# Where buffers lie in SBUF: weights on multiples of 256 bytes, activations 192 bytes past one

## The chip, the core and the metric

The kernel runs on one core of one Trainium2 chip. The metric is device time in microseconds of one execution, lower is better. Before the change it is 1898.5 us, the median of three runs (1892.57 to 1910.38).

## What is computed

Two transformer blocks over 256 tokens of width 1024, all in fp32. The first has two layers, each a token mixer and a convolutional FFN; the second is one layer with three kinds of attention over latent and context tokens, followed by a mixture of 32 experts. Cut to what matters:

```python
def first_block(x, ...):
    h = x
    for layer in range(DEPTH):                     # 2
        h = h + _token_mixer(_rmsnorm(h, norm1[layer]), w_in[layer], ...)   # xn @ w_in, attention, pooling, w_a, w_b, w_o
        h = h + _conv_ffn(_rmsnorm(h, norm2[layer]), w_up[layer], ..., w_down[layer])
    return _rmsnorm(h, norm_f)

def second_block(x, c, ctx, ...):
    mod_l = silu(c) @ w_ada + b_ada                # modulation, also for the context
    pl, pc = hl @ w_in, hc @ w_in                  # latent and context tokens
    ...                                            # hgrn2, rwkv7, neighbourhood attention
    xl = xl + g1l * (concat(a_lat, b_lat, c_lat) @ w_out)
    return xl + g2l * hierarchical_moe(h2l, ...)   # 32 experts, gate, up and down
```

## The kernel before

A linear layer keeps fp32 accuracy by splitting both factors into a high part in the format fp32r and the remainder. Activations are split once and kept as two tiles: xg (the normed input, two tiles), po, at and mgt in the mixer, hid in the FFN, hc for the context tokens, hl for the latent tokens, mx for the last projection. Weights are split as they arrive: `load` (line 338) brings a tile of 128 x 1024 through SP's queue into pool wr (three buffers), ACT writes its high part wh (line 348), DVE the remainder wl (line 349), and `mm3` issues three matmuls for each of eight slices of 128 rows: wh with the high activation (line 355), wh with the low one (356), wl with the high one (357). Weights are the stationary operand and activations move, 256 columns a matmul, 24 matmuls a weight tile. In `lin_tm` (w_v, w_i, w_nv) it is the other way about: activations are stationary and the weight moves, 512 or 256 columns.

The order of work is that of the program. Stages by time: mixer of layer 0 to 295 us, FFN-up to 492, FFN-down to 553; layer 1: mixer to 846, FFN-up to 1009, FFN-down to 1096; the second block's latent work to 1416; the experts from there. A generator of background work (`pump`) puts pieces of the second block's context work between them: `ada` (w_ada), `context_h` and `context1` in layer 0, `na_table` in FFN-down of layer 0 (a loop over eight heads of a load, two GpSimd operations and a store with two buffers), `ada` and `context2` in layer 1. Expert weights come in 96 tiles of 2 MB through SP's queue (line 1755), as the pools of the second block give their space back.

SBUF is given out by pools: those on the left are stacked upwards from the bottom, those with `side="right"` downwards from the top, tiles in a pool in the order of their first use, everything rounded up to 32 bytes. wh is two pairs of buffers (hi, lo); from the first FFN to the last a third pair, pool wh1 on the right side, takes every third weight tile (`s.whs = s.whs * 2 + [...]`). The addresses that follow from the sizes, with their place modulo 256 bytes (the slices of a tile are a multiple of 256 bytes apart, so that all slices share it):

```
tile(s)                      first byte(s) before               mod 256     after, by the diff
wr (w), wh, wl               34368, 46656, 54848 ...            64          0
wh1 (third pair)             142816, 146912                     224         0
xg, po / qk, mgt, hid / at   167904, 176096 / 184288 / 221152   224         192
hc (context)                 63040, 71232                       64          192
hl (latent)                  146176, 154368                     0           192
mx (high, low)               30144, 32256                       192, 0      128, 192
activation less weight:      xg, po, mgt, hid, at with wh 160, with wh1 0;
                             hc with wh 0, with wh1 96; hl with wh 192; mx with wh 128 and 192
```

## Time and profile before

| | |
|---|---|
| median of three runs | 1898.5 us (1892.57 to 1910.38) |
| the profiled execution | 1901.4 us |
| its span, first to last instruction | 1899.6 us |
| TensorE busy | 1746.7 us of the span |
| VectorE busy | 1097.6 us |
| ScalarE busy | 691.1 us |
| bytes read from HBM | 429.40 MB |
| mean granted TensorE clock | 0.960 |

PE is TensorE's matmuls, PEld its weight loads (they overlap the matmuls), DVE is VectorE, ACT ScalarE, POOL GpSimd, SP SyncE. A line number L355 is one of the kernel's. Matmuls are pipelined and their ends are modelled, so the length of one (0.28 us) is longer than the interval from its start to the next one's start; rates are read from starts.

### The profile page before, as it was taken

What the parts mean: (1) busy time and instruction counts of PE and PEld (TensorE: products, weight loads), DVE (VectorE), ACT (ScalarE), POOL (GpSimd) and SP (SyncE); (2) the same over time, 40 slices, a digit from 0 to 9 for tenths busy, and PEclk for the clock granted to TensorE, in tenths of its full rate; (3) what the DMA queues carried; (4) which work ended last, traced back from release to release, by engine and by line L of the source; (5) the groups of instructions that cost most, each with busy time, mean ns of one, the idle gap of its engine ahead of it and who ended that gap; (6) DMA issues with size and microseconds to landing.
All of it is one profiled execution on the core that took longest, in us unless ns stands there. A gap on an engine that the chain in (4) does not pass through costs nothing.

```text
span 1899.6 us, 37672 instructions
## 1 busy us (share of the span) xinstructions
PE 1746.7 (92%) x15846; PEld 1494.9 (79%) x15846; DVE 1097.6 (58%) x2087; ACT 691.1 (36%) x1078; POOL 148.3 (8%) x295
## 2 busy tenths in 40 slices
PE   7999999999989999999999979989998889878776
PEld 6879999999988889999999978976776555534443
DVE  5558568998545456588997579883544211211111
ACT  3346445654443355454553335421532000000000
POOL 2600000000230000000000001120001000000000
PEclk9999999999999999999999989975998999999999
DMA  9855455556667867454443443320339999999997
GB/s 306 262 186 165 162 190 183 180 176 212 213 223 264 284 215 230 149 165 136 155 158 128 138 156 127 111 68 11 111 148 380 426 427 425 426 427 425 426 425 290
DMA packets 94705, 441.14 MB, mean 232 GB/s; under 512 B 23796, under 2 KB 26388, under 8 KB 81728
## 3 DMA queue, kind: packets, MB, share of 16 engines
q1 hardware_dynamic: 90496, 432.17, 61.9%
q0 software_dynamic: 2224, 5.19, 1.1%
q8 instruction: 126, 2.06, 0.5%
q10 hardware_dynamic: 1808, 1.30, 0.2%
q14 instruction: 51, 0.42, 0.1%
HBM read 429.40 MB, written 9.20 MB: 231 GB/s over the span
## 4 chain that ended last, share of the span: by engine, by line
PE 57%; DMA 18%; DVE 6%; issue 2%; ACT 1%; POOL 1%; ACTq 0%; SPq 0%; POOLq 0%; DVEq 0%
PE g L355 8%; PE g L357 8%; PE g L356 8%; DMA we<-in_w_exp_up 6%; DMA we<-in_w_exp_gate 4%; DMA we<-in_w_exp_down 4%; PE g L1929 3%; PE acc L1953 2%; PE acc L357 2%; PE acc L355 2%; PE acc L356 2%; DVE wl L349 1%; PE g L1946 1%; PE sj L355 1%; PE sj L356 1%
## 5 line engine op out<-in xcount | busy, mean ns | idle before, releaser
L349 DVE TENSOR_TENSOR wl<-w,wh 128x1024 fp32r<-128x1024 f32 x347 | 428.1, 1235 | 244.0 <-ACT wh L348 238.9
L348 ACT ACTIVATE wh<-w 128x1024 fp32r<-128x1024 f32 x347 | 366.6, 1059 | 508.8 <-PE g L356 229.0
L355 PE MATMUL g<-xg,wh 128*128 128x256 f32 x1472 | 420.0, 285 | 13.1 <-ACT wh L348 13.0
L357 PE MATMUL g<-xg,wl 128*128 128x256 f32 x1472 | 419.2, 285 | 2.9 <-DVE wl L349 2.7
L356 PE MATMUL g<-xg,wh 128*128 128x256 f32 x1472 | 416.7, 283 | 0.5 <-DVE xg L504 0.4
L355 PEld LDWEIGHTS g<-xg,wh 128*128 128x128 f32 x1472 | 279.9, 190 | 20.0 <-ACT wh L348 13.9
L357 PEld LDWEIGHTS g<-xg,wl 128*128 128x128 f32 x1472 | 279.7, 190 | 12.6 <-DVE wl L349 5.5
L356 PEld LDWEIGHTS g<-xg,wh 128*128 128x128 f32 x1472 | 279.8, 190 | 4.7 <-issue 2.7
L1929 PEld LDWEIGHTS g<-we,xt 128*32 128x32 f32 x4096 | 109.7, 110 | 47.2 <-issue 27.1
L1929 PE MATMUL g<-we,xt 128*32 128x128 f32 x4096 | 126.4, 274 | 16.1 <-DMA we<-in_w_exp_up 15.3
L1935 DVE SCALAR_TENSOR_TENSOR hd<-hd,g 128x128 f32<-128x128 f32 x32 | 9.2, 288 | 216.0 <-ACT hd L1934 216.0
L1953 PE MATMUL acc<-dn,S 128*128 128x512 f32 (+1 forms) x264 | 120.6, 590 | 0.0
L1950 DVE TENSOR_TENSOR dn<-g,g2r 128x512 f32<-128x512 f32 (+1 forms) x66 | 44.6, 675 | 92.2 <-PE g L1946 90.0
L1946 PE MATMUL g<-we,ht 128*32 128x512 f32 (+1 forms) x528 | 69.7, 650 | 26.8 <-DMA we<-in_w_exp_down 17.7
L1934 ACT ACTIVATE hd<-g 128x128 f32<-128x128 f32 x32 | 8.9, 277 | 212.5 <-PE g L1929 212.5
L1953 PEld LDWEIGHTS acc<-dn,S 128*128 128x128 f32 x264 | 46.7, 192 | 41.8 <-issue 40.7
L1918 POOL TENSOR_SCALAR gr<-G,comb 128x128 f32<-128x128 f32 x64 | 38.0, 606 | 502.1 <-PE g L1922 354.3
L1924 ACT ACTIVATE S<-g 128x256 f32<-128x256 f32 x32 | 12.3, 384 | 155.9 <-PE g L1922 155.9
L355 PE MATMUL sj<-hl,wh 128*128 128x256 f32 x200 | 58.8, 294 | 6.7 <-ACT wh L348 5.5
L357 PE MATMUL sj<-hl,wl 128*128 128x256 f32 x200 | 58.0, 291 | 1.0 <-DVE wl L349 0.9
L356 PE MATMUL sj<-hl,wh 128*128 128x256 f32 x200 | 58.7, 293 | 0.1
L1946 PEld LDWEIGHTS g<-we,ht 128*32 128x32 f32 x528 | 15.5, 114 | 54.0 <-issue 40.5
(801 smaller groups left out, 3614.1 us busy)
## 6 DMA issues: line engine op xcount, KB each, us to landing
w<-in_w_in SPq DMA_DIRECT2D x135, 512.0 KB, 4.0
we<-in_w_exp_gate SPq DMA_DIRECT2D x32, 2048.0 KB, 38.5
we<-in_w_exp_up SPq DMA_DIRECT2D x32, 2048.0 KB, 39.1
we<-in_w_exp_down SPq DMA_DIRECT2D x31, 2048.0 KB, 35.4
w<-in_w_up SPq DMA_DIRECT2D x88, 512.0 KB, 3.3
wa<-in_w_ada SPq DMA_DIRECT2D x48, 512.0 KB, 5.4
w<-in_w_down SPq DMA_DIRECT2D x44, 512.0 KB, 3.4
w<-in_w_v SPq DMA_DIRECT2D x24, 512.0 KB, 3.4
```

The costliest lines, as they stand in the source:

```text
L348: s.nc.scalar.activation(hi, t, AF.Copy)
L349: s.nc.vector.tensor_tensor(lo, t, hi, op=OP.subtract)
L355: mm(out, w[0], x[0], start=first, stop=False, skip_group_check=sk)
L356: mm(out, w[0], x[1], start=False, stop=False, skip_group_check=sk)
L357: mm(out, w[1], x[0], start=False, stop=last, skip_group_check=sk)
L1918: nc.gpsimd.tensor_scalar(gr[:, i], G[:, i, e % 4, None, :].to_broadcast([128, 4, 32]), s.comb[:, i, e:e + 1], None, op0=OP.mult)
L1924: nc.scalar.activation(S, p[:, :T], AF.Copy)
L1929: nc.tensor.matmul(p[32 * j:32 * j + 32, q * 128:(q + 1) * 128], xt[:, k, (e % 4) * 32:(e % 4) * 32 + 32], w[:, k, j * 128:(j + 1) * 128], ...
L1935: nc.vector.scalar_tensor_tensor(hd[:, 0], hd[:, 0], 1.0, p[:, 0:128], op0=OP.add, op1=OP.mult)
L1946: nc.tensor.matmul(p[32 * c:32 * c + 32, :w], ht[:, c * 32:(c + 1) * 32], wd[:, c, q * w:(q + 1) * w], start=True, stop=True, tile_positio ...
L1950: nc.vector.tensor_tensor(dn, p[:, :w], s.g2r[:, q * w:(q + 1) * w], op=OP.mult)
L1953: nc.tensor.matmul(y[i][q * w // 512][:, o:o + w], S[:, i * 128:(i + 1) * 128], dn, start=(more and e == 0), stop=(e == 31), skip_group_ch ...
```

## The change

It alters where tiles lie, and no operation. `pad0` (128 bytes) is put at the bottom of the left side and `pad1` (224 bytes) at the top of the right side. vecs, the first constants, mean, zero, one1, mod, g1m and g2m become slices of one tile `small` whose size is a multiple of 256 bytes; lbt, hw0, ha0, wrt and brt become slices of a longer consts1. Pool sq gets a small tile `pads`, pool s1 one of 192 bytes at its beginning (`shift`) and one of 64 at its end (`unshift`), pool hcp one of 192 at its beginning. With that wr, wh and wh1 begin at a multiple of 256, and xg, po, qk, mgt, hid, at, hc and hl 192 bytes past one (the right column of the table above).

```diff
@@ -121,6 +121,7 @@
     _VOFF[(_n, _l)] = _o
     _o += _k
 NVEC = _o
+NSMALL = -(-(NVEC + _NC[0] + 123) // 64) * 64
 
 
 def _cols(w, tiles=None):
@@ -301,34 +302,44 @@
 
     def setup(s):
         nc = s.nc
+
+        s.pool("pad0").tile([128, 32], F32, name="pad0")
+        s.pool("pad1", side="right").tile([128, 56], F32, name="pad1")
         s.cp = s.pool("const")
         s.left, s.lw = ExitStack(), ExitStack()
         s.b2 = s.pool("b2", ctx=s.left)
         s.open_ps("1")
         s.dr = s.pool("dr", space=DRAM)
         s.hT = s.cp.tile([128, 8, T], F32, name="hT")
-        s.vecs = s.cp.tile([128, NVEC], F32, name="vecs")
+        small = s.cp.tile([128, NSMALL], F32, name="small")
+        cut = [0]
+
+        def take(n):
+            cut[0] += n
+            return small[:, cut[0] - n:cut[0]]
+        s.vecs = take(NVEC)
+        s.consts = [take(_NC[0]), s.b2.tile([128, -(-(_NC[1] + 344) // 64) * 64], F32, name="consts1")]
         nc.scalar.dma_start(s.vecs, s.a["vecs"])
         nc.sync.dma_start(s.hT[:, :4], s.a["xT"][:, :4])
         s.sq = s.pool("sq", bufs=2, ctx=s.left)
+        s.sq.tile([128, 16], F32, name="pads")
         s.wr = s.pool("wr", bufs=3, ctx=s.lw)
         s.whs = [s.pool("wh", bufs=2, ctx=s.lw)]
         s.first = s.wsplit(s.a["w_in0"][8], 8)
         nc.sync.dma_start(s.hT[:, 4:], s.a["xT"][:, 4:])
-        s.consts = [(s.b2 if i else s.cp).tile([128, _NC[i]], F32, name=f"consts{i}") for i in range(2)]
         nc.scalar.dma_start(s.consts[0], s.a["consts0"])
         s.ones = s.cp.tile([128, 128], F32, name="ones")
         nc.vector.memset(s.ones, 1.0)
-        s.mean = s.cp.tile([128, 1], F32, name="mean")
+        s.mean = take(1)
         nc.vector.memset(s.mean, 1.0 / D)
-        s.zero = s.cp.tile([128, 1], F32, name="zero")
+        s.zero = take(1)
         nc.vector.memset(s.zero, 0.0)
-        s.one1 = s.cp.tile([128, 1], F32, name="one1")
+        s.one1 = take(1)
         nc.vector.memset(s.one1, 1.0)
         s.ident = s.c("ident")
-        s.mod = s.cp.tile([128, 48, 2], F32, name="mod")
-        s.g1m = s.cp.tile([128, 2, 8], F32, name="g1m")
-        s.g2m = s.cp.tile([128, 8], F32, name="g2m")
+        s.mod = take(96).rearrange("p (k i) -> p k i", i=2)
+        s.g1m = take(16).rearrange("p (i k) -> p i k", i=2)
+        s.g2m = take(8)
 
 
 
@@ -492,6 +503,10 @@
                     t2[:, None, ::-1].to_broadcast([128, 8, 16]),
                     m2[:, :, None].to_broadcast([128, 8, 16]), op=OP.add)
 
+    def shift(s, pool, k):
+
+        pool.tile([128, k // 4], F32, name="shift")
+
     def norm_begin(s, gn, gl):
 
         s.nx = ([s.s1.tile([128, 8, T], F32R, name=f"xg{q}", tag=f"xg{q}") for q in range(2)], gn, gl)
@@ -513,6 +528,8 @@
         v = s.s1.tile([128, 2, 1536], F32, name="v", tag="v")
         att = s.s1.tile([128, 2, 4, T], F32R, name="at", tag="at")
         at = [att[:, q_] for q_ in range(2)]
+        if l == 0:
+            s.s1.tile([128, 16], F32, name="unshift")
         ps = [s.pair([w_in[8 + m] if l or m else s.first, w_in[9 + m]], x) for m in (0, 2)]
         rc, rows = s.token_r()
         rb = s.bc2(rows)
@@ -713,6 +730,7 @@
         nc = s.nc
         with ExitStack() as ctx:
             s.s1 = s.pool("s1", ctx=ctx, side="right")
+            s.shift(s.s1, 192)
             s.fp = s.pool("fp", bufs=2, ctx=ctx, side="right")
             bd = s.bd = s.dr.tile([128, 4096], F32, name="biasd")
             c1 = [ExitStack(), ExitStack()]
@@ -728,7 +746,7 @@
             for k in range(8):
                 s.norm_tile(k)
             s.bias_tables()
-            nc.sync.dma_start(s.consts[1], s.a["consts1"])
+            nc.sync.dma_start(s.consts[1][:, :_NC[1]], s.a["consts1"])
             nc.gpsimd.dma_start(bd, s.bias.rearrange("p h i c -> p (h i c)"))
             for l in range(2):
                 s.mixer(l)
@@ -779,7 +797,7 @@
         nc.vector.tensor_copy(s.identr, s.ident)
 
         l = s.col("hgrn_lb_logits_2", None, 4)
-        e = b2.tile([128, 3, 4], F32, name="lbt")
+        e = s.consts[1][:, _NC[1]:_NC[1] + 12].rearrange("p (a b) -> p a b", a=3)
         nc.vector.tensor_tensor(e[:, 0], l, l, op=OP.subtract)
         nc.scalar.activation(e[:, 0], e[:, 0], AF.Exp)
         nc.vector.reciprocal(e[:, 1], e[:, 0])
@@ -787,17 +805,17 @@
         nc.vector.tensor_tensor(e[:, 0], e[:, 1], e[:, 1], op=OP.subtract)
         nc.vector.tensor_scalar(e[:, 1], e[:, 0], -1.0, 1.0, op0=OP.mult, op1=OP.add)
         s.lb, s.lb1 = e[:, 0], e[:, 1]
-        s.hw0 = b2.tile([128, 4], F32, name="hw0")
+        s.hw0 = s.consts[1][:, _NC[1] + 12:_NC[1] + 16]
         nc.vector.tensor_scalar(s.hw0, s.col("rwkv_w0_2", 0, 4), 0.5, None, op0=OP.mult)
-        s.ha0 = b2.tile([128, 4], F32, name="ha0")
+        s.ha0 = s.consts[1][:, _NC[1] + 16:_NC[1] + 20]
         nc.vector.tensor_scalar(s.ha0, s.col("rwkv_a0_2", 0, 4), 0.5, None, op0=OP.mult)
         s.hS = [b2.tile([128, 2, 128], F32, name=f"hS{d}") for d in range(2)]
         s.rH = [[b2.tile([128, 128], F32, name=f"rH{d}{j}") for j in range(2)] for d in range(2)]
         for t in s.hS + s.rH[0] + s.rH[1]:
             nc.gpsimd.memset(t, 0.0)
         s.scp = b2.tile([128, 8, 32], F32, name="scp")
-        s.wrt = b2.tile([128, 8, 36], F32, name="wrt")
-        s.brt = b2.tile([128, 36], F32, name="brt")
+        s.wrt = s.consts[1][:, _NC[1] + 20:_NC[1] + 308].rearrange("p (k c) -> p k c", k=8)
+        s.brt = s.consts[1][:, _NC[1] + 308:_NC[1] + 344]
         s.nkv, s.rxd = s.dram("nkv", 2048), s.dram("rxd", 4096)
 
     def dram(s, n, k):
@@ -1511,6 +1529,7 @@
 
         nc = s.nc
         s.hcp = s.pool("hcp", ctx=s.chc)
+        s.shift(s.hcp, 192)
         hi, lo = s.hc = [s.hcp.tile([128, 8, T], F32R, name=f"hc{q}", tag=f"hc{q}") for q in range(2)]
         for q in range(2):
             xc = s.load(s.a["ctxT"][:, 4 * q:4 * q + 4].rearrange("p k t -> p (k t)"))
```

## Rows read from the trace of the kernel before

**Rows 1.** The page: span, and busy time (share) and instructions by engine.
```profile
span 1899.6 us, 37672 instructions
PE 1746.7 (92%) x15846; PEld 1494.9 (79%) x15846; DVE 1097.6 (58%) x2087; ACT 691.1 (36%) x1078; POOL 148.3 (8%) x295
```
**Rows 2.** Busy time by stage: stretch, its length, engines, granted clock, DMA share, GB/s.
```profile
0.00:100.00 100.00, 86.52 (x724) 75.74 (x724) 53.94 (x98) 35.58 (x52) 40.90 (x76) 1.00 0.89 287
100.00:295.00 195.00, 188.85 (x1363) 177.46 (x1364) 129.73 (x208) 102.51 (x149) 0.72 (x10) 0.98 0.52 171
295.00:492.00 197.00, 193.07 (x1562) 189.98 (x1561) 174.90 (x315) 110.72 (x148) 1.75 (x26) 0.99 0.56 188
492.00:553.00 61.00, 57.57 (x467) 56.00 (x466) 26.25 (x21) 22.02 (x22) 27.45 (x24) 1.00 0.70 213
553.00:846.00 293.00, 288.20 (x2284) 260.34 (x2283) 180.29 (x280) 136.87 (x194) 3.13 (x20) 1.00 0.67 223
846.00:1009.00 163.00, 159.90 (x1355) 158.38 (x1353) 152.48 (x282) 88.03 (x129) 3.60 (x24) 0.99 0.46 151
1009.00:1096.00 87.00, 86.80 (x742) 86.49 (x742) 50.22 (x90) 26.98 (x34) 1.49 (x3) 1.00 0.40 132
1096.00:1416.00 320.00, 298.82 (x1932) 251.09 (x1932) 227.72 (x538) 125.70 (x230) 31.20 (x48) 0.85 0.29 98
1416.00:1885.00 469.00, 381.04 (x5384) 235.68 (x5383) 99.11 (x255) 41.16 (x121) 38.02 (x64) 0.96 0.99 416
```
**Rows 3.** The page: the chain that ended last, by engine and by line.
```profile
PE 57%; DMA 18%; DVE 6%; issue 2%; ACT 1%; POOL 1%; ACTq 0%; SPq 0%; POOLq 0%; DVEq 0%
PE g L355 8%; PE g L357 8%; PE g L356 8%; DMA we<-in_w_exp_up 6%; DMA we<-in_w_exp_gate 4%; DMA we<-in_w_exp_down 4%; PE g L1929 3%; PE acc L1953 2%; PE acc L357 2%; PE acc L355 2%; PE acc L356 2%; DVE wl L349 1%; PE g L1946 1%; PE sj L355 1%; PE sj L356 1%
```
**Rows 4.** Timeline of SP from 1415 us: start, length, queue, line, operation.
```profile
1416.29 0.33 SPq L1755 DMA_DIRECT2D we<-in_w_exp_down  x1
```
**Rows 5.** The page: costliest groups, busy time and mean ns, then idle time before.
```profile
L355 PE MATMUL g<-xg,wh 128*128 128x256 f32 x1472 | 420.0, 285 | 13.1 <-ACT wh L348 13.0
```
**Rows 6.** Timeline of PE in the FFN-up stage of layer 0: four matmuls' starts.
```profile
399.77 0.28 PE L356 MATMUL g<-xg,wh 128*128 128x256 f32 x1
...
401.33 0.28 PE L357 MATMUL g<-xg,wl 128*128 128x256 f32 x1
401.45 0.28 PE L355 MATMUL g<-xg,wh 128*128 128x256 f32 x1
...
406.97 0.28 PE L357 MATMUL g<-xg,wl 128*128 128x256 f32 x1
```
**Rows 7.** Timeline of PE, latent stage: first and last of 68 matmuls.
```profile
1120.15 0.28 PE L356 MATMUL sj<-hl,wh 128*128 128x256 f32 x1
...
1128.04 0.28 PE L357 MATMUL sj<-hl,wl 128*128 128x256 f32 x1
```
**Rows 8.** Timeline of PE, latent stage: first and last of 114 matmuls.
```profile
1135.86 0.28 PE L355 MATMUL sj<-hl,wh 128*128 128x256 f32 x1
...
1148.67 0.28 PE L357 MATMUL sj<-hl,wl 128*128 128x256 f32 x1
```
**Rows 9.** Line 355 alone by stage: stretch, length, PE and PEld, clock, DMA.
```profile
0.00:100.00 100.00, 55.27 (x192) 36.93 (x192) 1.00 0.89 287
```
**Rows 10.** Busy time in the middle of FFN-up of layer 1, as rows 2.
```profile
900.00:950.00 50.00, 50.00 (x430) 50.00 (x429) 49.03 (x84) 26.61 (x36) 0.39 (x6) 1.00 0.47 157
```
**Rows 11.** The chain in order of time from 495 us: start, length, what.
```profile
500.32 4.18 DMA z<-in_na_rpb
...
541.46 5.82 DMA z<-in_na_rpb
...
554.58 5.92 DMA w<-in_w_in
```
**Rows 12.** Timeline from 294 us: a reader and a later writer of xg.
```profile
294.69 0.28 PE L355 MATMUL g<-xg,wh 128*128 128x256 f32 x1
...
296.81 0.49 ACT L503 ACTIVATE xg<-hT,vecs 128x256 fp32r<-128x256 f32 x1
```

## The prediction

> **What bounds the kernel now.** I read the page's busy row first: TensorE is busy nine tenths of the span [rows 1], but a busy PE is not yet a bound. The table by stage says where it is one [rows 2]. It has three kinds of stretch. Up to 1096 us (the two layers of the first block) PE works without a break and DVE trails it, closely in the two stages at 295 and 846 us. From 1096 to 1416 us small matmuls of the second block follow one another at a clock of 0.85 on average. From 1416 to 1885 us the DMA share is 0.99: the expert weights stream in, and nothing but their bytes sets the pace. The chain of waits agrees [rows 3]: 57% PE, 18% DMA, and the largest PE groups are the three lines of `mm3`. The expert stream is let go at 1416 us by an issue that stands in SP's queue behind the second block [rows 4]; so what is saved before 1416 us moves the whole stream forward, and what is saved after it is worth nothing.
>
> The change issues no operation more or less, so the question is how fast the matmuls of lines 355 to 357 follow one another. Each has 256 columns; the groups give its modelled length, 285 ns [rows 5], which overlaps the next. What counts is the interval from start to start, and the reader gets it from two rows and the number between them.
>
> **The interval depends on two addresses.** Write "distance" for the position of the moving tile (activation) less that of the stationary tile (weight), modulo 256 bytes; the table of addresses above gives both. In one FFN-up stage, with the same xg throughout, a weight buffer of pool wh1 (distance 0) gives 13 intervals in 1.56 us, exactly 120.0 ns each; from 401.45 us the next buffers belong to wh (distance 160), and 47 intervals take 5.52 us, 117.4 ns [rows 6]. Only the weight buffer changed; engine, stage and neighbours did not. The latent stage of the second block already has distance 192, the one the change makes everywhere. There I find two steady beats: 67 intervals in 7.89 us, 117.8 ns [rows 7], and 113 intervals in 12.81 us, 113.4 ns [rows 8]. A run keeps its beat until PE next has to wait. Of the 180 intervals of these two runs, the longest of the stage, 113 are fast; I take two thirds, so 2/3 x 113.4 + 1/3 x 117.8 = 114.9 ns is the mean I expect at distance 192.
>
> **The change, part by part.** *Weights to 0, activations to 192.* By the loops, the first mixer has 68 weight tiles of 24 such matmuls (the 12 tiles of w_v are 512 wide and have the weight as moving operand), all at distance 160: 1632 matmuls, each 117.4 - 114.9 = 2.5 ns shorter. From the first FFN on the three pairs of buffers take turns, one at distance 0 and two at 160: (5.1 + 2 x 2.5)/3 = 3.4 ns. The context projections (14 tiles, mostly distance 0) gain about 5 ns. The sum on PE alone:
> mixer 0: 1632 x 2.5 = 4.1 us (576 of them before 100 us, from 192 of line 355 [rows 9]: 1.4 us; the rest 2.7);
> FFN-up 0 with the context: 1056 x 3.4 + 336 x 5 = 5.3;
> FFN-down 0: 528 x 3.4 = 1.8;
> mixer 1: 1632 x 3.4 = 5.5;
> FFN-up 1: 1056 x 3.4 = 3.6;
> FFN-down 1: 1.8. Together 22.1 us.
> The hl and mx matmuls keep their distances (192; 128 and 192) and are worth nothing.
>
> How much of it reaches the end is read stage by stage [rows 2]. Before 100 us the DMA share is 0.89 and weights set part of the pace: half, 0.7. Mixer 0 after that has DVE idle for a third: all, 2.7. FFN-up 0 has DVE at 174.9 of 197 us: half, 2.7. FFN-up 1 has 152.5 of 163, and 49.0 of 50 us in its middle [rows 10]: a PE that is 3% faster wants more than DVE has there, so wl, which PE needs, comes late next: half, 1.8. FFN-down 0 ends with the chain of `na_table` from 500 to 554 us (DMA, POOL, DMA, eight heads), behind which the w_in loads of the next layer wait on SP [rows 11]: nothing. Mixer 1 and FFN-down 1 in full: 5.5 and 1.8. Sum 15.2 us of 22.1.
>
> *Bounds.* If every run took the slow beat (117.8), distance 160 loses 0.4 ns and distance 0 gains 2.2: -0.7 + 4800 x 0.47 ns + 336 x 2.2 ns = 2.3 us, of which the same share is 1.6. If every run took the fast beat (113.4): 1632 x 4.0 + 4800 x 4.9 + 336 x 6.6 = 32.3 us, of which 22. I choose the mixture, since rows 7 and 8 are the very distance.
>
> *The w_v and w_nv matmuls* (512 columns, weight moving) go from distance 96 or 0 to 64; there are some 340, and with 7 ns, the largest spread of rows 6 to 8, either way they are worth at most 2.4 us; I take 0. *fp32 matmuls*: about 1,350 records remain before 1096 us (the rows of the seven stages less three times line 355's share); at 7 ns they would be worth 9 us up or down; I take 0, since in most of them both operands lie in pools that move together. *Pads, `small`, the tail of consts1*: no instruction, no DMA and no queue position is added; 56 to 192 bytes each, so no pool is pushed out. If `small` brought a wait, the DVE instruction that writes mod would hold everything behind it (see the rivals). *DMA into shifted tiles*: the expert stream has 0.99 of its engines and cannot get faster; bound 0 to 1% of 469 us, 5 us, taken as 0.
>
> The profiled execution took 1901.4 us (span 1899.6 and 1.8 around it), 2.9 us above the median of the runs shown. 1901.4 - 15.2 = 1886; against the median, 1898.5 - 15.2 = 1883. I forecast 1883.
>
> **A rule against the change.** The row shows two intervals, 120.0 and 117.4, that differ by the weight buffer's place alone [rows 6]. The Trainium skill, page "SBUF — State Buffer", section "Who interferes with whom", says that TensorE reads the moving operand and the next weights through two independent ports and that it never waits on anyone. By that rule no placement matters and the sum is 0; by the rows it is 15 us. The rows speak against it, within one stage. The page "TensorE: Matmul & The Clock Gate", section "Back-to-back issue gap", puts an isolated matmul of 256 columns at 256/2.4 + 2.5 = 109 ns; as an estimate from it, 6,768 matmuls at 109 would give some 60 us on PE, but no run of rows 6 to 8 gets there.
>
> **Rivals.**
> *A. The fast beat everywhere.* In the layers the runs are longer than in the latent stage, and once all buffers share one distance a run crosses from tile to tile without a jolt. If the fast beat is the one that lasts, 22 us: 1876. For it: the longest run of the latent stage is the fast one [rows 8]. Against: the slow one is just as steady for 67 intervals [rows 7].
> *B. Little or nothing arrives.* Either placement is not what sets the interval (the skill's rule above as a mechanism: ports independent, latent stage faster for another reason), then 1898; or the slow beat wins or DVE, nearly full in two stages [rows 2, 10], takes back what PE gains: 2 to 8 us, 1890 to 1897. Against the first stands the switch within one stage [rows 6].
> *C. Slower: waits through `small`.* mod, vecs, ident and the constants now lie in one tile. If order were kept for the tile as a whole, each of the six writes of mod (line 842) and the two of g1m would wait for all reads of ident and vecs before it, on PE behind up to a pair of weight tiles: 48 x 0.12 = 5.8 us a time, 8 times 46 us, less 15: 1929. It turns into a loss from three such waits on. Against: order goes by slices: PE reads the first slices of xg at 294.69 while ACT writes later slices of the same tile at 296.81 [rows 12].
>
> **Chances.** Forecast (both beats, 10 to 20 us) 0.50; A (20 to 30 us) 0.24; B 0.20; C and anything else that is slower 0.06. A measurement of this kernel tells about 1%, 19 us, from no change (its runs lie 18 us apart). Faster by over 1% means more than 19 us: A and a small part of the forecast, 0.30. Slower by over 1% is C, 0.05. Within 1%: 0.65. The range reaches from 1868 (A, with the fp32 bound partly in its favour) to 1899 (nothing arrives); it leaves out the rest of the fp32 bound and C. The likeliest case alone: 1878 to 1889.
>
> **What would show it.** Right: the mean of lines 355 to 357 falls from 285 ns towards 276 to 281; in FFN-up intervals of 113.4 or 117.8 and no 120.0 any more; the expert stream starts 12 to 18 us before 1416; DVE's busy share in FFN-up 1 nears all of it, with idle time of PE before line 357; `na_table` still takes 55 us. Wrong: intervals as before (rule of independent ports); PE waiting on DVE by more than 8 us in the layers (B); waits before line 842 and before readers of ident (C); a longer stretch at half clock between 1096 and 1416 us, which would hide any of it.

## The result and the profile after

The changed kernel takes 1878.1 us (median of six runs, 1872.9 to 1882.6) beside 1895.5 us for the kernel before (six runs too; the 1898.5 ahead of the prediction is the median of three of them): a ratio of 0.9885, 95% interval 0.9839 to 0.9930. Run twice more, unaltered, on other occasions, it gave 0.9892 (0.9845 to 0.9939) and 0.9902 (0.9868 to 0.9935). The medians differ by 17.4, 22.9 and 20.0 us. The forecast was 15.2 us (1883), with 1868 to 1899 as the range. Single executions can fall into a slower state with a lower granted clock, as two of e10's twelve did; e10's time below is the median of the other ten.

The page of the changed kernel: span, busy time by engine, and the groups that answer to [rows 1, 5]. Its lines 366, 367, 368 are the 355, 356, 357 of before, 359 and 360 the two halves of the split.

```profile
span 1876.3 us, 37673 instructions
PE 1726.2 (92%) x15846; PEld 1476.6 (79%) x15846; DVE 1096.1 (58%) x2087; ACT 691.3 (37%) x1078; POOL 149.5 (8%) x295
...
L366 PE MATMUL g<-xg,wh 128*128 128x256 f32 x1472 | 417.6, 284 | 13.2 <-ACT wh L359 13.2
L368 PE MATMUL g<-xg,wl 128*128 128x256 f32 x1472 | 416.8, 283 | 4.1 <-DVE wl L360 3.8
L367 PE MATMUL g<-xg,wh 128*128 128x256 f32 x1472 | 414.1, 281 | 0.0
```

Same operations, 20.5 us less busy PE. The mean lengths of the three groups hardly move (285, 283 and 285 ns before for lines 355, 356 and 357; 284, 281 and 283 now); a length includes a modelled end. The intervals from start to start, which carry the argument, can't be seen here.

They can in the timeline of PE, FFN-up stage of layer 0 (start, length, line, operation): first and last of two unbroken runs of the changed kernel.

```profile
337.08 0.28 PE L367 MATMUL acc<-hc,wh 128*128 128x256 f32 x1
...
352.83 0.28 PE L368 MATMUL g<-xg,wl 128*128 128x256 f32 x1
...
366.06 0.28 PE L367 MATMUL acc<-hc,wh 128*128 128x256 f32 x1
...
384.68 0.28 PE L366 MATMUL acc<-hc,wh 128*128 128x256 f32 x1
```

The first holds 139 intervals in 15.75 us, 113.3 ns each; the second 158 in 18.6 us, 117.8 each. They are the two beats of [rows 7, 8], and both runs cross from hc to xg and from weight tile to weight tile without a change. The 120.0 of [rows 6] is gone. Over all of the about 6,900 unbroken intervals at distance 192 and full clock the mean is 115.1 ns, and the same for the layers and the context alone. In the profile before it was 117.8 at distance 160 (about 4,550) and 119.6 at distance 0 (about 1,760), together 118.3.

Busy time by stage of the changed kernel, columns as in [rows 2], with stretches cut at the new boundaries; the last row is the middle of FFN-up 1, as [rows 10].

```profile
0.00:100.00 100.00, 86.67 (x732) 75.62 (x733) 56.95 (x102) 36.87 (x54) 42.08 (x76) 1.00 0.90 288
...
292.00:488.00 196.00, 190.82 (x1573) 187.63 (x1572) 173.83 (x314) 108.84 (x145) 1.75 (x26) 0.99 0.57 192
...
840.00:1001.00 161.00, 157.80 (x1347) 156.35 (x1347) 149.51 (x278) 85.70 (x124) 3.58 (x24) 0.98 0.45 148
...
886.00:936.00 50.00, 50.00 (x443) 50.00 (x442) 49.93 (x87) 27.50 (x38) 0.52 (x8) 1.00 0.49 161
```

In the middle of FFN-up 1 PE does 443 matmuls in 50 us where it did 430; DVE goes with it, 87 operations for 84, and now has 49.93 us of the 50.

SP's timeline at the release of the expert stream (answers to [rows 4]), and the chain of `na_table` in order of time (answers to [rows 11]; start, length, what).

```profile
1394.95 0.33 SPq L1774 DMA_DIRECT2D we<-in_w_exp_down  x1
```
```profile
492.71 6.70 DMA z<-in_na_rpb
...
532.62 6.20 DMA z<-in_na_rpb
...
546.19 6.12 DMA w<-in_w_in
```

The stream starts 21.3 us earlier. The chain from the first table load to the next layer's w_in takes 53.5 us (54.3 before): it began 7.6 us earlier, and the w_in load behind it came 8.4 us earlier.

**Where the time came from.** To mark the stages I take the start of the last or first matmul that reads a certain tile, in two profiles of the kernel before (the second is the run e8) and three of the kernel after (e7 and e12). Lengths in us, one value for each profile:

| stage | before | after | gain of the means | forecast |
|---|---|---|---|---|
| mixer 0 | 284.7, 283.4 | 278.8, 279.9, 279.3 | 4.7 | 3.4 |
| FFN-up 0 | 197.4, 197.7 | 195.2, 194.7, 196.2 | 2.2 | 2.7 |
| FFN-down 0 and wait for w_in | 72.6, 77.0 | 72.6, 73.5, 73.4 | 1.6 | 0 |
| mixer 1 | 284.4, 285.3 | 279.2, 279.3, 279.7 | 5.5 | 5.5 |
| FFN-up 1 | 160.5, 164.1 | 157.4, 161.1, 161.0 | 2.5 | 1.8 |
| FFN-down 1 | 84.9, 87.4 | 85.3, 86.0, 85.9 | 0.4 | 1.8 |
| latent, first to last hl | 158.0, 160.1 | 157.5, 157.7, 157.9 | 1.3 | 0 |
| latent, last hl to first mx | 125.2, 109.5 | 120.5, 109.5, 106.5 | (clock) | 0 |

Up to the latent stage that is 16.9 us. The two mixers are steady from profile to profile, within 1.3 us; the FFN stages vary by up to 4.4 us for the same kernel. The last row is no effect of the change, as e7 and e8 show.

Much of the spread of the FFN stages is the clock. FFN-up 1 in the first profile before and in e8, the same kernel, then in the first profile after and in e7 (columns as in [rows 2]; the clock is the third number from the end):

```profile
849.00:1009.60 160.60, 157.50 (x1333) 155.86 (x1331) 150.08 (x278) 87.25 (x127) 3.60 (x24) 0.99 0.46 151
```
```profile
853.30:1017.40 164.10, 161.00 (x1332) 159.27 (x1330) 150.66 (x278) 87.19 (x127) 3.59 (x24) 0.97 0.45 149
```
```profile
835.60:993.00 157.40, 154.20 (x1332) 152.54 (x1330) 149.83 (x278) 87.25 (x127) 3.58 (x24) 0.99 0.47 156
```
```profile
837.30:998.40 161.10, 158.12 (x1333) 156.26 (x1331) 150.38 (x279) 87.31 (x127) 3.59 (x24) 0.96 0.45 153
```

PE ran at 1.2 GHz for 3.4, 11.4, 3.4 and 12.0 us of these, and there an interval takes 213 ns, so about half of that time is lost. An estimate with half of it taken off: FFN-up 1 is 158.8 and 158.4 us before, 155.7, 155.1 and 154.8 after, a gain of 3.4; FFN-down 1 is 84.9 and 84.6 before, 83.6, 83.5 and 83.5 after, a gain of 1.2; FFN-up 0 gains 2.7. The first part of the latent stage gains nothing (146.3 and 145.7 before; 146.3, 146.3 and 146.6 after), so its 1.3 us go with the clock.

### The profile page after: what moved, and what is told of

Its sections match the earlier page's. It is cut to its first block, busy times and chain, and to the rows that moved or that the text cites. A ratio compares the mean times of both kernels' runs of the same rounds, so it can differ in the third digit from the quotient of the medians.

```text
span 1876.3 us, 37673 instructions
## 1 busy us (share of the span) xinstructions
PE 1726.2 (92%) x15846; PEld 1476.6 (79%) x15846; DVE 1096.1 (58%) x2087; ACT 691.3 (37%) x1078; POOL 149.5 (8%) x295
## 4 chain that ended last, share of the span: by engine, by line
PE 55%; DMA 19%; DVE 7%; issue 2%; ACT 1%; POOL 1%; SPq 0%; ACTq 0%; POOLq 0%; DVEq 0%
PE g L366 8%; PE g L368 8%; PE g L367 8%; DMA we<-in_w_exp_up 6%; DMA we<-in_w_exp_gate 4%; DMA we<-in_w_exp_down 4%; PE g L1948 3%; PE acc L1972 2%; PE acc L368 2%; PE acc L366 2%; PE acc L367 2%; DVE wl L360 2%; DMA w<-in_w_in 1%; PE g L1965 1%; DMA z<-in_na_rpb 1%
## 5 line engine op out<-in xcount | busy, mean ns | idle before, releaser
L366 PEld LDWEIGHTS g<-xg,wh 128*128 128x128 f32 x1472 | 279.7, 190 | 19.8 <-ACT wh L359 13.8
L367 PEld LDWEIGHTS g<-xg,wh 128*128 128x128 f32 x1472 | 279.9, 190 | 4.2 <-issue 2.7
```

The lines of the kernel that those rows point to most:

```text
L366: mm(out, w[0], x[0], start=first, stop=False, skip_group_check=sk)
L367: mm(out, w[0], x[1], start=False, stop=False, skip_group_check=sk)
```

## The experiments

All ratios are to runs of the kernel before on the same chip. Mean intervals are worked out from the starts in each run's trace: three-product matmuls of 256 columns in the layers and the context, unbroken, at full clock.

**e1: matmuls alone.** A stream with nothing beside it, at 14 pairs of places.

```python
for rep in range(5):
    for wo, xo in PAIRS:          # offsets of weights and activations
        p = ps.tile([128, 512], F32, name="p", tag="p")   # one buffer
        ... 16 x mm3 on hi/lo[wo + ...], x0/x1[xo + ...]
        nc.vector.tensor_scalar(z[...], p[...], 0.0, None, op0=OP.mult)
```

> This kernel leaves out the whole computation and writes zeros: it holds only runs of 48 fp32r matmuls in the pattern of mm3, with nothing beside them, at 14 pairs of places (weight, activation, in bytes past a multiple of 256), each five times, with a short wait before every run. Theory D (the distance activation minus weight, modulo 256, sets the interval): start-to-start 120.0 ns at distance 0, about 117.4 at 160, two beats of 113.4 and 117.8 at 192, and the pairs (64,0), (128,64), (32,224), which are also at 192, as (0,192). Rival P (two independent ports, placement is nothing, the intervals of the kernel come from other engines beside PE): one interval for all 14 pairs, under 113 ns. Rival Q (the absolute place of the weight counts): (64,0) and (128,64) differ from (0,192).

Timeline of PE, e1: first and last matmul of 39 intervals at distance 0, then at 192 (the first eight intervals of each run are left out).

```profile
99.32 0.28 PE L2046 MATMUL p<-x,lo 128*128 128x256 f32 x1
...
104.00 0.28 PE L2046 MATMUL p<-x,lo 128*128 128x256 f32 x1
...
137.14 0.28 PE L2046 MATMUL p<-x,lo 128*128 128x256 f32 x1
...
141.56 0.28 PE L2046 MATMUL p<-x,lo 128*128 128x256 f32 x1
```

4.68 us against 4.42: 119.9 and 113.3 ns. By distance:

| distance, bytes | 0 | 32 | 64 | 96 | 128 | 160 | 176 | 192 | 208 | 224 | 240 |
|---|---|---|---|---|---|---|---|---|---|---|---|
| ns | 119.9 | 116.6 | 113.3 or 117.8 | 119.9 | 118.7 | 117.4 | 119.2 | 113.3 | 119.1 | 118.3 | 117.2 |

At 64 two of the five runs took 117.8 and three 113.3. The pairs (64, 0), (128, 64) and (32, 224), all at distance 192, gave 113.3 like (0, 192). So the distance modulo 256 sets the interval and the absolute place doesn't; neither the DMA nor another engine is needed. The Trainium skill, page "SBUF — State Buffer", section "Who interferes with whom", has TensorE read both operands through independent ports and wait for no one; this stream doesn't bear that out for its own two operands, 113.3 to 119.9 ns by place alone.

**e2, e3, e4: one part of the layout undone or moved.** Edits of the changed kernel. e2 takes the shift away; e3 moves weights and activations together by 64 bytes; e4 puts one of three weight pairs at distance 0.

```diff
# e2 (each line from another place)
-            s.shift(s.s1, 192)
-        s.shift(s.hcp, 192)
-            s.s1.tile([128, 16], F32, name="unshift")
+            s.s1.tile([128, 64], F32, name="unshift")
# e3
-        s.pool("pad0").tile([128, 32], ...); s.pool("pad1", ...).tile([128, 56], ...)
+        s.pool("pad0").tile([128, 48], ...); s.pool("pad1", ...).tile([128, 40], ...)
# e4, ahead of the line that makes wh1
+                    s.pool("padw", ctx=ctx, side="right").tile([128, 16], F32, name="padw")
```

> The changed kernel with activations of the linear layers at 0 as the weights, so that all of them but hl and mx are at distance 0 and not at 192. Theory D: 120.0 ns in all of them; 6,800 x 4.9 ns is 33 us on PE, of which the trace of after shows three quarters arriving: about 1903 us, ratio to the kernel before 1.004 (1.000 to 1.008). Rival (multiples of 256 bytes are good by themselves, the 192 is decoration): as after, ratio 0.9885.

> The changed kernel with everything 64 bytes further on both sides: weights at 64, activations at 0, all distances as in after. Theory D: as after, ratio to the kernel before 0.9885 (0.984 to 0.993), same mean interval of 115 ns. Rival Q (the weights' place on a multiple of 256 counts): the gain is lost, ratio 0.995 to 1.000.

> The changed kernel with the third pair of weight buffers alone moved to 192, which puts it at distance 0 again: one tile in three from the first FFN on. Theory D: 1,600 matmuls at 120.0 in place of 115.1, 7.8 us on PE, three quarters of it 6 us: ratio to the kernel before 0.992. Rival (what counts is only that most tiles are well placed, since DVE holds the pace in the FFN): as after, 0.9885.

| kernel | mean interval, ns | median, us | ratio (95%) |
|---|---|---|---|
| e2, distance 0 | 119.8 | 1899.2 | 0.9999 (0.9972 to 1.0027) |
| e3, all moved by 64 | 115.1 | 1878.3 | 0.9905 (0.9867 to 0.9942) |
| e4, one pair at 0 | 117.2 | 1887.1 | 0.9948 (0.9924 to 0.9972) |

Without the shift nothing of the gain is left, with all multiples of 256 kept; moved as a whole the layout keeps it; one pair back at 0 takes about half. Two of the three expectations missed. e2 was to be 0.4% slower than the kernel before and took the same time, although its first hl matmul starts at 1122.5 us, 7.1 later than the mean of the two profiles of the kernel before; where that goes was not found. e4 was to lose less (0.992), because only one tile in three was counted. The trace shows what was left out. Four starts of one unbroken run of e4: its first, the first on the pair at distance 0, the first back at 192, its last.

```profile
389.22 0.28 PE L366 MATMUL acc<-hc,wh 128*128 128x256 f32 x1
...
394.32 0.28 PE L366 MATMUL g<-xg,wh 128*128 128x256 f32 x1
...
397.19 0.28 PE L366 MATMUL g<-xg,wh 128*128 128x256 f32 x1
...
402.73 0.28 PE L368 MATMUL g<-xg,wl 128*128 128x256 f32 x1
```

The 45 intervals before the tile at 0 take 113.4 ns, the 24 on it 119.9, the 47 after it 117.8, and PE never waits. Of the 43 stretches at 192 (16 intervals and more) that PE entered in this way from a tile at 0, 42 ran at the slow beat; of the 90 others 54 ran at the fast one. So the two good pairs fell from 115.1 to 116.5 ns on average, nearly half of e4's loss on PE. One badly placed buffer costs the well-placed ones too.

The costliest group of e2 and of e3, from their pages (columns as above):

```profile
L366 PE MATMUL g<-xg,wh 128*128 128x256 f32 x1472 | 425.5, 289 | 16.5 <-ACT wh L359 16.4
```
```profile
L366 PE MATMUL g<-xg,wh 128*128 128x256 f32 x1472 | 417.7, 284 | 13.5 <-ACT wh L359 13.5
```

**e5: what chooses the slow beat at 192?** In the changed kernel about 4,030 intervals belong to runs at 113.3 and 2,270 to runs at 117.8 (runs of 20 and more), and none changes beat before its next wait. e5 was to lay splits and DMA loads beside the stream, and tries all pairs of distances for the two activation halves apart. Two accumulators take turns, so PE doesn't wait between runs.

```diff
-        ps = ...tile_pool(name="ps", bufs=1, space=PSUM)
+        ps = ...tile_pool(name="ps", bufs=2, space=PSUM)
+        for rep in range(24): run(*hl, 192, 192)          # fixed weights
+        for rep in range(24): run(*split(), 192, 192)     # new weights each run
+        for rep in range(24): ...two 512 KB loads...; run(*split(), 192, 192)
+        for rep in range(3):
+            for d1, d2 in PL: run(*split(), d1, d2)
```

> This kernel leaves the whole computation out and writes zeros: its time says nothing. It issues 285 runs of 48 of the three-product fp32r matmuls (128x128 weights, 256 columns) on two fixed activation tiles. Parts: distances 184, 188, 196, 200, 60, 64, 68 bytes with fixed weights, 3 runs each; distance 192, 24 runs with fixed weights; distance 192, 24 runs whose weights are split anew before each run by ScalarE (copy) and VectorE (subtract) into two rotating buffers, as in the kernel; 24 more with a load of 1 MB by DMA beside each; then all 64 pairs of distances in steps of 32 bytes for the two activation halves apart (first half from the weights: d1, second half: d2), 3 runs each with split weights. Question: why a third of the kernel's intervals at distance 192 are 117 to 118 ns and not 113.3. Theory S (the beat of a run is chosen by how it starts, on the waits for the split halves): the 24 fixed runs are all at 113.3, of the 24 split runs some 4 to 14 at 117.8. Theory L (the slow beat comes from DMA traffic beside PE): split runs at 113.3 without DMA, some at 117.8 with it, beginning and ending within a run. For the 64 pairs: those with d1 not equal to d2 lie between the means of d1 = d2 (113.3 to 120); a mean under 113.3, or 113.3 in all runs of a pair where (192, 192) isn't always fast, would be a better layout.

Neither came: all 72 runs at (192, 192) took 117.8 ns, the first 24 with nothing beside them but VectorE's short reading of the accumulator. So the slow beat needs no neighbour, and Theory L falls. The loads don't bear on it: nothing made them wait for the runs they were written beside, and all were over in the first 82 us, during the runs at 184 to 68 bytes. The first 82 us and the 24 runs with loads (columns as in [rows 2], the DMA share is the last but one):

```profile
0.00:82.00 82.00, 72.25 (x585) 71.96 (x586) 5.57 (x15) 7.29 (x7) 0.20 (x4) 1.00 0.86 327
403.90:539.50 135.60, 135.60 (x1154) 135.60 (x1153) 33.98 (x48) 25.42 (x24) 0.00 (x0) 1.00 0.00 1
```

The runs at 188, 196 and 200 bytes took the same 118.7, 121.8 and 120.0 ns under these loads and, a third time, without them. Theory S couldn't be tested: the stream never stopped, so the beat it fell into after the runs at 68 bytes stayed for 72 runs. Of the 64 pairs none was below 116.9. Places next to 192 are worse: 188 gives 118.7, 196 gives 121.8, 184 and 200 give 120.0.

**e6: a wait before every run**, of three kinds.

```diff
+        def run(d1, d2, kind):
+            if kind != "acc":
+                nc.scalar.activation(y[:, 32:64], y[:, :32], AF.Copy)    # ACT waits for the run before
+                nc.scalar.activation(hi[:, :256], w[:, :256], AF.Copy)
+            if kind == "lo":
+                nc.vector.tensor_tensor(lo[:, :256], w[:, :256], hi[:, :256], op=OP.subtract)
+            ...                                                           # 24 matmuls, one accumulator
```

> This kernel leaves the whole computation out and writes zeros: its time says nothing. 576 runs of 24 of the three-product fp32r matmuls, every one begun after a wait of one of three kinds: for the accumulator (acc), for the first weight half, rewritten by ScalarE (hi), for both halves, the second by VectorE, so that PE stops again at the third matmul (lo). All 64 pairs (d1, d2) of distances in steps of 32 bytes, three times each. In the kernel after the change every unbroken stretch at distance 192 keeps one beat from its first matmuls to the next wait: of 133 stretches some two thirds 113.3 ns, the others 117.8. Theory S (the start chooses): at (192, 192) runs begun on acc are at 113.3, as in the first bare stream, where all 20 were; among hi and lo some are at 117.8; within a run the beat doesn't change after the first ten matmuls. Theory L (something beside PE sets it): all nine at 113.3, since nothing runs beside. For the other pairs: where d1 = d2 the means of the first stream again (119.9 at 0, 116.6 at 32, 113.3 or 117.8 at 64, 119.9 at 96, 118.7 at 128, 117.4 at 160, 118.3 at 224) on acc. A pair with 113.3 in all nine runs where (192, 192) has some at 117.8 would be worth some 10 us in the kernel (2334 intervals by 4.4 ns).

Timeline of PE, e6, distance 192: matmul 12 and matmul 24 of three runs, begun on the accumulator, on the first weight half, on both.

```profile
574.74 0.28 PE L2057 MATMUL p<-x,lo 128*128 128x256 f32 x1
...
576.15 0.28 PE L2057 MATMUL p<-x,lo 128*128 128x256 f32 x1
...
578.14 0.28 PE L2057 MATMUL p<-x,lo 128*128 128x256 f32 x1
...
579.50 0.28 PE L2057 MATMUL p<-x,lo 128*128 128x256 f32 x1
...
581.50 0.28 PE L2057 MATMUL p<-x,lo 128*128 128x256 f32 x1
...
582.86 0.28 PE L2057 MATMUL p<-x,lo 128*128 128x256 f32 x1
```

Twelve intervals in 1.41, 1.36 and 1.36 us: 117.8, 113.3, 113.3, the same in all three repetitions, with nothing beside PE once a run has begun. Theory S holds in its main point, the start chooses the beat and it stays, but its guess which start is slow was the wrong way round: the accumulator's start was slow here and fast in e1, where the matmul before it differed. At distance 64 the accumulator and the first half begin fast, both halves slow. In all 64 pairs only (64, 64) and (192, 192) ever ran at 113.3; no other pair of 32-byte steps was below 116.6.

**e7, e8, e9: the two kernels again, and distance 64.** e7 and e8 are unaltered. e9 is the changed kernel with 64 for 192.

```diff
-            s.shift(s.s1, 192)
+            s.shift(s.s1, 64)
-        s.shift(s.hcp, 192)
+        s.shift(s.hcp, 64)
-            s.s1.tile([128, 16], F32, name="unshift")
+            s.s1.tile([128, 48], F32, name="unshift")
```

> The changed kernel once more, unaltered, for a second profile and a tighter ratio. Theory N: the stretch of half clock in the latent stage (61 us long in the profile before, 51 in the first profile after, 27 in the three variants profiled so far) is not tied to the placing of tiles but to the execution; then this profile has another length of it than 51 us, most likely 27, the stage from the last hl matmul to the first mx matmul takes about 109.5 us and not 120.5, and the profile's span is some 1864 to 1868 us; up to the first hl matmul the marks are within 1 us of the first profile after (288.6, 483.8, 556.4, 835.6, 993.0, 1094.1 us). Theory T (the kernel's own timing sets it): 51 us and 120.5 us again. The ratio of times is expected at 0.9885 (0.984 to 0.993).

> The kernel before once more, unaltered, for a second profile. Theory N (the latent stage's half-clock stretch belongs to the execution): another length than 61 us, most likely 27, the stage from the last hl to the first mx matmul about 109.5 us instead of 125.2, the span some 1884 us. Theory T (the kernel's own timing): 61 us and 125.2 us again. Up to the first hl matmul the marks within 1 us of the first profile (294.6, 492.0, 564.6, 849.0, 1009.6, 1110.2 us), which says how exactly gains by stage can be read from one profile.

> All activations of the linear layers 64 bytes past the multiple of 256 (distance 64) and not 192; only the sizes of the shifts are changed. In the bare streams 64 and 192 are the only distances with the 113.3 beat, each with 117.8 as its other beat, chosen by the start. Theory S (two distances, same two beats): the mean interval in the kernel is between 113.3 and 117.8, the time within 0.5 % of the kernel after: ratio to before 0.984 to 0.993; which of 64 and 192 gets the fast beat more often is left to the starts: by the bare streams 64 begins fast on a wait for the accumulator or the first weight half and slow on one for the second half, so a share of fast stretches of about a half to three quarters is expected. If 192 had something of its own, the ratio would be that of the slow beat everywhere (117.8 and not 115.1, some 12 us of the gain gone: 0.995).

The latent stage from the last hl to the first mx: the first profile of the kernel before, then e8, the same kernel (columns as [rows 2]).

```profile
1268.00:1394.00 126.00, 122.76 (x610) 88.06 (x609) 63.07 (x159) 43.68 (x98) 5.39 (x6) 0.76 0.22 64
```
```profile
1280.00:1391.00 111.00, 107.76 (x616) 80.04 (x613) 63.52 (x161) 43.58 (x98) 5.39 (x6) 0.88 0.25 74
```

Same kernel, same work, 15.7 us apart, at a mean clock of 0.76 and 0.88: the stretch at 1.2 GHz was 61 us long in the one and 27 in the other. After gave 51, 27 and 20. Its length belongs to the execution, so the 4.7 us that the first pair of profiles shows there are no gain of the layout. The marks missed their 1 us: e8 reached the first hl 10.4 us later than the first profile of the same kernel, e7 6.1 us later. The spans missed with them (e7 1872.7 us for 1864 to 1868, e8 1897.6 for 1884). Only means over profiles can be read by stage, and the clock of each stage has to be looked at first.

e9 gave 1888.7 us, ratio 0.9952 (0.9922 to 0.9983), mean interval 117.5 ns. Of its intervals in long runs at distance 64, some 5,500 were at about 118 and some 400 at 113.3. The time is the one that the rival of that expectation gave, but not for its reason: 192 and 64 have the same two beats, but in this kernel's order of waits 64 nearly always starts in the slow one.

**e10, e11, e12: is it the distance alone?** e10 is the kernel before with three pads that put all activations at 192; e11 is the changed kernel with the old distances; e12 the changed kernel beside them.

```diff
# e10, against the kernel before (each line from another place)
+        s.pool("pad1", side="right").tile([128, 56], F32, name="pad1")
+                    s.pool("padw", ctx=ctx, side="right").tile([128, 48], F32, name="padw")
+        s.hcp.tile([128, 48], F32, name="shift")
# e11, against the kernel after
-            s.shift(s.s1, 192)
+            s.shift(s.s1, 160)
-        s.shift(s.hcp, 192)
-            s.s1.tile([128, 16], F32, name="unshift")
+            s.s1.tile([128, 24], F32, name="unshift")
+                    s.pool("padw", ctx=ctx, side="right").tile([128, 24], F32, name="padw")
```

> The kernel before with three padding tiles and nothing else of the change: all activations of the linear layers at distance 192 from all weight buffers (weights at 64 mod 256, activations at 0), the small tiles, constants and the first addresses as before. Why: set against the mean interval of the fp32r matmuls (119.8 ns at distance 0, 117.5 at 64, 117.1 with one pair at 0, 115.1 at 192), the ratios measured (0.9999, 0.9952, 0.9948, 0.9892) lie on a line of 0.00225 per ns that passes 0.9965, not 1, at the 118.3 ns of the kernel before: some 6 us of the gain may belong to another part of the change (Theory R: the rest of the layout gives 6 us). Theory D (distance alone, the line's offset is spread of the measurements): ratio 0.989, as the changed kernel of the same batch. Theory R: 0.9925, 6 us above it. Mean interval 115.1 ns under both.

> The changed kernel with the distances of the kernel before: activations at 160, the third weight pair also at 160 (distance 0), the context's activations at distance 0; all else of the change kept. Mean interval 118.3 ns. Theory D (distance alone): ratio to before 1.000, within 0.997 to 1.003. Theory R (the rest of the layout gives some 6 us): 0.9965, with the interval under 1.

> The changed kernel unaltered, beside the two others on the same chip, so that they can be set against it directly. Expected ratio to before 0.989 (0.985 to 0.993), mean interval 115.1 ns. With the half-clock stretch of the latent stage at 27 us, as in six of eight profiles so far, the span is 1870 to 1877 us.

| kernel | mean interval, ns | median, us | ratio (95%) |
|---|---|---|---|
| e10, distance 192 in the old layout | 114.9 | 1878.8 | 0.9914 (0.9883 to 0.9944) |
| e11, old distances in the new layout | 118.3 | 1895.3 | 0.9973 (0.9937 to 1.0010) |
| e12, the change | 115.4 | 1877.5 | 0.9902 (0.9868 to 0.9935) |

Three pads without the other edits bring 18.7 of 20.0 us. The new layout with the old distances is 2.2 us faster than the kernel before by the medians, which its interval can't tell from nothing. The times alone don't settle Theory R: e10's interval holds its 0.9925 as well as Theory D's 0.989, and e11's holds its 0.9965. The marks speak for D. e11 reaches the first hl at 1115.2 us, the kernel before at 1110.2 and 1120.6; e10 reaches it at 1093.6, the changed kernel at 1094.1, 1100.2 and 1101.1. A few us from the rest of the layout stay possible and unresolved. No run was measurably faster than the changed kernel.

## Why the prediction was right, point by point

**Distance sets the interval: right, and shown.** e1 gives it with PE alone, e2 takes the gain away, e3 shows that only the difference of the places counts, e10 brings most of the gain with the distance alone. Why the distance matters, no run here shows. The first half of rival B (another cause, 1898) falls, and with it the rule of independent ports as a mechanism for this kernel.

**Both beats, two thirds fast: right.** Forecast mean 114.9 ns, measured 115.1, 115.2 and 115.4; 64, 63 and 58% of the intervals in long runs are fast where 67% was put. That it came so close is partly luck: the two thirds were read from two runs of another stage, and e9, which has the same two beats, is slow in more than nine intervals of ten. Rival A (the fast beat everywhere) falls by the stretches at 117.8, one of them 158 intervals long, in the timeline above. Runs do cross tiles, and while all of these lie at one distance the beat changes only at a wait; four in five of these matmuls had the same beat in all three profiles of the changed kernel, so the waits don't draw it at random.

**The sum on PE: right.** Forecast 22.1 us. Some 6,350 unbroken intervals of the layers and the context at 118.3 - 115.1 = 3.2 ns give 20.3 us, and busy PE fell by 20.5.

**How much of it arrives: too little by about 5 us against the times.** The forecast of 15.2 stands against 16.9 at the first hl mark and 20.1 as the mean of the three differences of medians. (The forecast time, 1883, is 4.9 us too high; 3.0 of that is the base, 1898.5 where six runs gave 1895.5.)

By its terms: *mixer 0*, 3.4 for 4.7. Its 576th matmul of lines 355 to 357 starts at 99.0 and 98.6 us before and at 98.1, 100.4 and 97.2 after, so of the 0.7 put into the first 100 us only 0.2 came on average. By the 627th, at about 120 us, the gain is 2.2, and the rest of the stage adds 2.6, where 2.7 was put. Most of the 2 us between may be the clock: the half-clock stretch there was 6.8 us long in both profiles before and 3.4, 0 and 6.8 after.

*Mixer 1* came out to the tenth, 5.5.

*FFN-up*, "half, DVE": 2.7 and 1.8 for 2.2 and 2.5 by the marks. The sum fits, the reason doesn't. In FFN-up 1, where DVE was fullest, the interval fell from 118.3 to 114.6 ns, 3.9 us over 1056 matmuls, and by the estimate with the clock 3.4 us arrived, not half; the 3.9 us are also all that PE gained in FFN-up 0 with the context (118.6 to 115.8 ns), where 5.3 was put and 2.2 to 2.7 arrived. DVE had 49.93 of 50 us, yet PE hardly waited for it. PE's waits for wl, from the waits of PE in the first profile before and the first after (waiter, what it waited for: us, times, longest):

```profile
PE g L357 <- DVE wl L349: 3.8, 6, 1.0
```
```profile
PE g L368 <- DVE wl L360: 4.9, 7, 1.0
```

So 1.1 us came on top and not some 4.

*FFN-down 0*, "nothing": 1.6, inside the 4 us by which the kernel before differs from itself there; its chain kept its length, as forecast. *FFN-down 1*, "in full, 1.8": 0.4 by the marks. The clock hides the rest: PE ran at 1.2 GHz for 0 and 5.6 us of it before and 3.4, 5.0 and 4.8 after, and the estimate without that is 1.2. The interval there fell only from 118.4 to 116.1 ns, because more of its runs take the slow beat, and 2.3 ns over 528 matmuls are 1.2 us too.

The 3.2 us between the 16.9 of the marks and the 20.1 of the times are not settled: the 1.3 in the first part of the latent stage go with the clock, e11's 2.2 us may belong to it, and so may the spread, since single executions of the kernel before lie up to 25 us apart (1890.1 to 1914.8 beside e7).

**Edits taken as nothing: right within the measurement.** Rival C asked for waits before the writes of mod. The line of these writes has the same wait behind it before and after, one of 0.4 us at a weight load, and the changed kernel has no slower stage. (The pads are 64 to 224 bytes by the diff, not 56 to 192; nothing hangs on it.) The 512-column matmuls were not quite nothing: those of w_v went from distance 96 to 64 and from 233.5 to 229.5 ns, 1 us over 240 of them. The commonest fp32 matmuls kept their interval, 216 ns for 256 columns.

**The chances: too low for "faster".** The bound of 1% lies at 19 us, and the three measurements gave 1.15, 1.08 and 0.98%. The forecast of 15 us put 0.65 on the wrong side of a bound that the result sits on. Taking half in FFN-up 1 because a second engine was nearly full made the middle too small; a stage in which DVE has 49 of 50 us still followed a PE that was 3% faster.

**What would show it: one sign was badly chosen.** The mean length of lines 355 to 357 was to fall to 276 to 281 ns; it fell by 1 to 2 ns, to 284, 281 and 283. The length of a matmul in the profile includes a modelled end and doesn't follow the interval. The idle time of PE before line 357 grew by only 1.1 us. The other signs came: no 120.0, both beats, DVE full, `na_table` at 54 us, and the expert stream earlier, by 21 us in the first pair of profiles, 5 of them from the clock. Its mean start over the profiles is 1414.7 before (two) and 1391.2 after (three).

## What to carry to other kernels

When fp32r matmuls of 256 columns follow one another without a stop, read the interval from start to start, not the mean length of the group, and set it against where the two operands begin modulo 256 bytes. Here 192 bytes from weights to activations is worth 3 to 5 ns of 120 on each, and a few bytes of padding set it. Place every buffer of a rotation, since one at distance 0 pulled its neighbours into the slow beat. Profile the kernel twice, and look at the clock of each stage, before reading gains of a few us: the same kernel differed from itself by 10 us at the same mark.

## What the runs showed of the hardware

- The interval of back-to-back fp32r matmuls (128x128 weights, 256 columns) at full clock runs from 113.3 to 121.8 ns by the distance of the operands modulo 256 bytes, with nothing else running (e1, e5). The Trainium skill, page "TensorE: Matmul & The Clock Gate", section "Back-to-back issue gap", gives 109 ns for an isolated one of 256 columns; no steady run here came below 113.3.
- At distances 64 and 192 the stream has two stable beats, 113.3 and 117.8 ns. The start after a wait chooses, and at one distance the beat then lasts until PE next waits: 306 intervals in a row in the kernel, 72 runs of 48 matmuls in e5. A tile at distance 0 on the way leaves the slow beat behind it (e4, 42 of 43).
- The same start is fast in one surrounding and slow in another (the accumulator's, e1 and e6). What in the start decides was not found.
- At 1.2 GHz the interval is 213 to 214 ns at distances 0, 64, 160 and 192 alike (the half-clock stretches of e8, e2, e9 and after), so the distance shows only at full clock.
- At 512 columns another distance is good: 228.5 ns at 0 (e2), 229.5 at 64 (after), 233.5 at 96 (before), 233.2 at 192 (e9), with the weight as the moving operand.
- The stretch at half clock (1.2 GHz) in the latent stage lasted 61 or 27 us for one kernel, and 51, 27 or 20 us for the other.
